# Two halves of the tensor engine in turn: the small fp32 products of an S5 mixer and of attention scores

## The chip, the cores and the metric

The kernel runs on one core of a Trainium2 chip. The metric is the device time of one execution in microseconds (us). A core has a tensor engine (PE, whose weight loads the profile calls PEld), a vector engine (DVE), a scalar engine (ACT), GpSimd (POOL), and SyncE (SP), which issues the DMAs here. Products are written to PSUM; the other engines read them from there.

## What is computed

The reference is a decoder trunk of two layers on 256 tokens of 1024 features. Cut to what matters:

```python
for i in range(DEPTH):                                   # 2
    x = layer_norm(ALPHA * x + 0.5 * swiglu(x, ...))      # feed-forward, 1024 -> 2816 -> 1024
    h = x @ w_in[i]
    z_gmlp, z_qk, z_v, z_s5, z_gate = split(h)
    y_a = gmlp_mixer(z_gmlp, ...)
    y_b = diff_attention(q, k, v, lam, ...)               # 4 heads, two score maps each, causal, 64-wide q and k
    y_c = s5_mixer(z_s5, ...)                             # 32 groups of 16 features, 64 complex states each
    mix = sum_k sigmoid(z_gate[k]) * ((y_a, y_b, y_c)[k] @ w_branch[i, k])
    x = layer_norm(ALPHA * x + mix @ w_out[i])
    x = layer_norm(ALPHA * x + 0.5 * swiglu(x, ...))
```

In `s5_mixer` an input product makes the states' inputs, a linear recurrence over the tokens makes the states, and an output product with a skip term makes y, which goes through a GELU and a gated linear unit (GLU).

## The kernel before, in words

**Products.** Nearly all products are with large weights. A weight tile is split into a high and a low part (`wh` on ACT, `wl` on DVE) and each product is done as three with inputs rounded to fp32r. The small products are left in plain fp32, and each of them stands in the trace as two MATMULs: the S5 input products `bu`, the S5 output products `py`, the attention scores `pss`, and the products with the attention weights `po`.

**Order.** The program has no loop order of its own. Streams (Python generators) yield operations, requests for buffers (`Alloc`) and `Event`s. `Scheduler.run` (L250) keeps a model of each engine's clock and of when each tile is written and read, and merges the streams into one static program; each engine then executes its instructions in that order, waiting on semaphores. A `bundle` (L70) is a group of operations of one engine that is issued without another between. On PE the small streams go ahead of the main stream once their inputs are due; the attention streams have priority 30, the S5 ones 40 (35 for the first step of the scan), the main stream 50.

**PSUM.** The small products share the pool `acc` of four banks (`ps`, L316). A bank comes free when its reader is through.

**The mixer** (L1153). After the products of gMLP, values and the S5 input, the main stream computes q and k (`psq`), then 12 gates (`psg`), four products of the first two branches (`psp`, from `ya` and `yb`), the GLU (`psl`) and the third branch (`psc`), in the order of the list `GATES`. Beside it run three S5 streams and two attention streams:

- `s5_in` (L1034), for each of four feature tiles f: for i = 0 and then i = 1, four products with rows 64 i to 64 i + 63 of `wbf` and `U`, into a bank `bu` of its own.
- `s5_scan` (L1052): DVE turns the inputs (`t`), scans them (`gr`, `gi`) and turns them back into `Hr` and `Hi`.
- `s5_out` (L1105), for each f: state products 64 columns wide with `Hr` (p = 0) and `Hi` (p = 1), for q2 = 0, 1 and i = 0, 1, output partitions 64 i to 64 i + 63; and a direct map for each q2 and i, 32 by 32, on rows 64 i to 64 i + 31 and output partitions 64 i + 32 to 64 i + 63. All of them go into one bank `py`, and the accumulation starts and ends for each q2. The bundles are (q2 = 0, p = 0): state, direct, state, direct; (0, 1): state, state; and the same for q2 = 1. ACT copies `py` into `y`, DVE adds the skip term, and for two tiles at a time GELU and a split give `y5h` and `y5l`, which the GLU reads.
- `head` (L960), one stream for the even and one for the odd heads (e = 0, 1), four heads-and-query-blocks n = 0 to 3 in turn: allocate one bank `pss`, two score products with rows 64 e to 64 e + 63 of q and k (128 keys wide for n = 0, 1; 256 for n = 2, 3), the softmax on DVE and ACT, transposes (`tra`), and `po`. A stream asks for the scores of n + 1 only after `po` of n. `heads_out` normalizes and transposes a query block and gives `ybh` and `ybl`.

Of the kernel before, what the change touches and what calls it, by code (L numbers as in the profile page):

```python
# [31 lines left out]
# The order of the gates (branch, pair of output tiles), of the products of the first two branches (3 + branch, half of  # L32
# the output tiles) and of the GLU.
# [3 lines left out]
# Priorities of the streams (smaller goes first).  # L37
# [8 lines left out]
# Activation tables that hold a function.  # L46
# [3 lines left out]
class Op:  # L50
    """Instructions of one engine that are issued together."""
# [5 lines left out]
class Alloc:  # L57
    def __init__(self, pool, tag, bufs, make):
        self.pool, self.tag, self.bufs, self.make = pool, tag, bufs, make

# [21 lines left out]
class Engine:  # L82
    """Turns a call into an Op with an estimate of its cost."""
# [40 lines left out]
class Scheduler:  # L124
    """Merges streams of operations into one program order.

    Every stream is a generator that yields Ops (issued in its order), Allocs (answered with a tile once a buffer is
    free) and Events (passed once set).  An estimate of each engine's clock and of when each piece of a tile is
    written and read decides which stream goes next."""

# [14 lines left out]
    def spawn(self, gen, prio):  # L145
        p = prio if callable(prio) else (lambda: prio)  # of the stream's other engines; on PE it precedes the main stream
        self.seq += 1
        self.streams.append([gen, p, None, self.seq])

# [73 lines left out]

    def free(self, *tiles):
        for t in tiles:
            name = t[:].tensor.name
            self.slots[self.where.pop(name)].append(float(self.track[name][0].max()))

# [1 line left out]
    def settle(self, s):  # L230
        gen = s[0]
        val = None
        while True:
            h = s[2]
            if isinstance(h, Op):
                return True
            if isinstance(h, Alloc):
                val = self.alloc(h)
                if val is None:
                    return True  # L240
            elif isinstance(h, Event):
                if not h.ok:
                    return True
            try:
                s[2] = gen.send(val)
            except StopIteration:
                return False
            val = None
# [31 lines left out]
class Pair:  # L280
    """Two chunks of the weights: as loaded, and split into two parts."""
# [5 lines left out]
class Trunk:  # L287
# [36 lines left out]
    def slab(self, i, tag, name, dt, bufs):  # L324
        # a pair of chunks, in the ring or in tiles that are idle then
        if i in self.spare:
            tags = self.spare[i].pop(0)
            h = []
            for tg in tags:
                x = yield self.t([128, 1024], tg, name, dt)  # L330
                h.append(x)
            return h, h
        x = yield self.t([128, 2048], tag, name, dt, bufs)
        return [x], [x[:, 0:1024], x[:, 1024:2048]]
# [52 lines left out]
    def xstat(self, out, x, t, pair, i, n):  # L387
        # token tile t of x @ 512 columns; K-tiles 4 i .. 4 i + 3 of 4 n
# [9 lines left out]
    def wstat(self, out, ws, x):  # L398
        # ws: (hi, lo) [128, 128] of each K-tile; out [128, 256]
# [9 lines left out]
    def blocks(self, w, c, j, n):  # L409
        # n K-tiles of 128 columns, from column block j of chunk c  # L410
        return [tuple(z[c][:, 128 * (j + k):128 * (j + k) + 128] for z in (w.hi, w.lo)) for k in range(n)]

    def couple(self, name):
        # two output tiles of the next pair of weight chunks
# [7 lines left out]
    def sums(self, final):  # L422
        # PSUM of a product with 1024 output columns: (columns, tile) for each token tile
# [9 lines left out]
    def kdown(self, acc, h, pair, t, first, last, only=None):  # L433
        # two K-tiles of a product with 1024 output columns, token tile t
# [18 lines left out]
    def rsqrt(self, out, v, eps, tmp):  # L453
        # 1 / sqrt(v + eps) by Newton's iteration; out, v, tmp: [128, 1]
# [8 lines left out]
    def rsqrt_w(self, out, v, eps, tmp):  # L463
        # the same for any width
# [8 lines left out]
    def stats(self, src, n, eps):  # L473
        # mean in column 0, 1 / deviation in column 2
# [8 lines left out]
    def to_xt(self, src, t, gain=None, done=None):  # L483
        # features of token tile t onto partitions, in two parts; gain: (scale, bias) by feature
# [79 lines left out]
    def affine(self, t, x, gb):  # L564
        # gain and bias of the normalized tokens, for the residual
# [18 lines left out]
    def tail(self, n, acc, h, xr, gb, final, first=False):  # L584
        # the last n pairs of K-tiles, token tile 0 ahead of token tile 1
        ps = []
        x_ev = [Event(), Event()]
        for t in range(2):
            if t == 1 and final:
                # by pieces of the columns, for the last normalization to start early  # L590
# [131 lines left out]
    def prep(self, layer, r):  # L722
        """r receives what the mixer of this layer needs."""
# [19 lines left out]
        # minus lambda of the differential attention  # L743
# [18 lines left out]
        # th - 2 pi round(th / 2 pi)  # L762
# [14 lines left out]
        # c = (a - 1) / lambda  # L777
# [13 lines left out]
        # block-diagonal input and output maps  # L791
# [48 lines left out]
        # C, then C a; the imaginary parts negated  # L840
# [23 lines left out]
        # transposes of the input maps, and the direct map of even tokens  # L864
# [25 lines left out]
        # rotation tables: cos and sin of 2 theta c, c = 16 a + b  # L890
# [69 lines left out]
    def head(self, r, qk, va, hs, st):  # L960
        V, A = self.V, self.A
        ts, stt = V.tensor_scalar, V.scalar_tensor_tensor
        for e in [r["ev"]] + st["in"]:
            yield e
        for qb, h in hs:
            ke = 128 * (qb + 1)
            rows = slice(64 * (h % 2), 64 * (h % 2) + 64)
            ps = yield self.ps(self.acc, "pss", (128, 2, 256))
            yield bundle([self.mmul(ps[:, m, 0:ke], qk[0][rows, 2 * m + h // 2, qb * 128:qb * 128 + 128],
                                    qk[1][rows, 2 * m + h // 2, 0:ke], True, True) for m in range(2)])  # L970
# [6 lines left out]
            self.free(ps)  # L977
            yield ts(out=a[:, 2:4], in0=a[:, 0:2], scalar1=-0.125, scalar2=None, op0=ALU.mult)
# [28 lines left out]
        if st["run"] == 0:  # L1007
            self.free(va, *qk)
# [25 lines left out]
    def s5_in(self, r, U2, ev_u, box):  # L1034
        # input products of the four feature tiles
        yield r["ev"]
        yield ev_u
        for f in range(4):
            wb = yield self.t([128, 2, 2, 128], "wbf", "wbf", bufs=2)
            yield self.GQ.dma_start(out=wb, in_=r["wbd"][f // 2][:, 2 * (f % 2):2 * (f % 2) + 2])  # L1040
            if f:
                yield box[f - 1][2]
            for i in range(2):
                rs = slice(64 * i, 64 * i + 64)
                x = yield self.ps(self.acc, f"bu{i}", (128, 2, 2, 128))
                yield bundle([self.mmul(x[:, p, q2, :], wb[rs, q2, p, :], U2[rs, 2 * f + q2, :], True, True)
                              for q2 in range(2) for p in range(2)])
                box[f][i].append(x)
                box[f][i][0].set()
# [55 lines left out]
    def s5_out(self, r, u5, U2, out):  # L1105
# [3 lines left out]
        for f in range(4):  # L1109
# [4 lines left out]
            for q2 in range(2):  # L1114
                j = 2 * f + q2
                for p in range(2):
                    ops = []
                    for i in range(2):
                        q = 2 * q2 + i
                        ops.append(self.mmul(py[64 * i:64 * i + 64, q2, :], cf[:, q, p, :], self.H[p][:, q, :],  # L1120
                                             p == 0, p == 1))
                        if p == 0:
                            ops.append(self.mmul(py[64 * i + 32:64 * i + 64, q2, 0:128],
                                                 r["k0"][64 * i:64 * i + 32, j, :], U2[64 * i:64 * i + 32, j, :],
                                                 False, False))
                    yield bundle(ops)
# [26 lines left out]
    def mixer(self, layer, r):  # L1153
# [57 lines left out]
        # gMLP  # L1211
# [28 lines left out]
        # attention  # L1240
# [13 lines left out]
        st = {"in": qk_ev + va_ev, "po": [None, None], "got": [None, None], "left": [4, 4], "run": 2, "o": o, "yb": yb, "n": 0, "ev": Event()}  # L1254
        for e in range(2):
            s.spawn(self.head(r, qk, va, [(0, e), (0, e + 2), (1, e), (1, e + 2)], st), P_ATT)
# [14 lines left out]
        # gates, and the products of the first two branches  # L1271
# [13 lines left out]
        def branch(b, m2):  # L1285
            # branch b, two pairs of output tiles
# [112 lines left out]
    def main(self):  # L1399
# [21 lines left out]
        def warm():  # L1421
            # keeps the clock of the tensor engine up until the first weights are there
# [59 lines left out]
def pack(inp):  # L1482
    """Lays the weights out in the order in which the tensor engine takes them, and the small arrays by partition."""
# [4 lines left out]
    def rows(w, c0, n):  # x-stationary operand: all K-tiles of n columns, 2048 columns of data per pair  # L1488
        v = w[:, c0:c0 + n].reshape(-1, 128, n).transpose(1, 0, 2)
        for i in range(0, v.shape[1], 4):  # L1490
            chunks.append(v[:, i:i + 4].reshape(128, 2048))

    def cols(w, c0, n):  # weight-stationary operand: tiles [K-tile, 128 columns]
# [43 lines left out]
    def states(v):  # [32 groups, 64 states, ...] -> [(2 groups, states), 16, ...]  # L1537
# [42 lines left out]
```

## Time and profile before

| | |
|---|---|
| median of 3 runs | 1253.62 us (1252.46 to 1255.15) |
| the profiled execution: span, first to last instruction | 1251.0 us |
| PE busy | 1236.9 us, 99% |
| PEld busy | 1140.3 us, 91% |
| DVE busy | 889.1 us, 71% |
| ACT busy | 636.4 us, 51% |
| DMA | 246.18 MB, mean 197 GB/s |

How to read it: busy time is the union of an engine's instructions. Matmuls overlap, so their mean duration is longer than the distance between their starts, and what a group of products costs is read from its first start to the start of what PE does next. The chain of work that ended last goes back from the last instruction to whatever released each step.

### The profile page before, as it was taken

How to read it: one execution, taken by the hardware profiler on the slowest of the kernel's cores; microseconds unless marked ns; L12 is line 12 of the kernel's file. 1: busy time of each engine (PE TensorE's matmuls, PEld its weight loads, DVE VectorE, ACT ScalarE, POOL GpSimd, SP SyncE). 2: the span in 40 equal slices, each digit the busy share in tenths (PEclk: the TensorE clock that was granted, in tenths of full speed). 3: DMA queues.
4: the chain of work that ended last, by engine and by line, in shares of the span. 5: the costliest groups of instructions: out<-in, count | busy, mean ns of one | idle time of the engine just before them, and what ended most of it. 6: DMA issues, size and time to landing. Idle time of an engine off the chain costs nothing.

```text
span 1251.0 us, 21124 instructions
## 1 busy us (share of the span) xinstructions
PE 1236.9 (99%) x8734; PEld 1140.3 (91%) x8734; DVE 889.1 (71%) x1564; ACT 636.4 (51%) x980; POOL 14.8 (1%) x52
## 2 busy tenths in 40 slices
PE   8999999999999999999999999999999999999997
PEld 7999998999999889999889999989998998999996
DVE  6887659769886898775685544695798778754546
ACT  6445537655635564454464343467464366543430
POOL 2000000000000020000000000000000000000000
PEclk9999999999999999999999999999999999999998
DMA  8657654653445565666455554465535464654540
GB/s 311 247 177 258 242 204 170 232 215 110 166 185 209 206 227 203 223 237 216 171 227 189 186 191 180 170 237 204 194 118 186 183 216 155 252 200 175 196 168 34
DMA packets 42864, 246.18 MB, mean 197 GB/s; under 512 B 4880, under 2 KB 5648, under 8 KB 17424
## 3 DMA queue, kind: packets, MB, share of 16 engines
q1 hardware_dynamic: 42768, 244.84, 53.8%
q8 instruction: 68, 1.11, 0.3%
q14 instruction: 28, 0.23, 0.1%
HBM read 233.28 MB, written 11.53 MB: 196 GB/s over the span
## 4 chain that ended last, share of the span: by engine, by line
PE 97%; DVE 2%; ACT 1%; DMA 0%; issue 0%; DVEq 0%
PE ac L196 23%; PE puc L196 17%; PE pgc L196 16%; PE psg L196 12%; PE psq L196 4%; PE psp L196 4%; PE pg L196 3%; PE pu L196 2%; PE py L196 2%; PE psc L196 2%; PE psu L196 2%; PE ps L196 2%; PE pvg L196 2%; PE pva L196 2%; PE bu L196 1%; PE pss L196 1%
## 5 line engine op out<-in xcount | busy, mean ns | idle before, releaser
L196 DVE TENSOR_TENSOR wl<-raw,wh 128x1024 fp32r<-128x1024 f32 (+2 forms) x416 | 481.2, 1189 | 189.1 <-ACT wh L196 174.9
L196 ACT CAST wh<-raw 128x1024 fp32r<-128x1024 f32 (+2 forms) x416 | 410.0, 1023 | 276.3 <-PE ac L196 92.6
L196 PE MATMUL pgc<-xl,wh 128*128 128x256 f32 x576 | 163.7, 284 | 0.0
L196 PE MATMUL puc<-xl,wh 128*128 128x256 f32 x576 | 163.3, 284 | 0.0
L196 PE MATMUL puc<-xh,wl 128*128 128x256 f32 x576 | 163.0, 283 | 0.0
L196 PE MATMUL puc<-xh,wh 128*128 128x256 f32 x576 | 163.0, 283 | 0.0
L196 PE MATMUL pgc<-xh,wl 128*128 128x256 f32 x576 | 163.0, 283 | 0.0
L196 PE MATMUL pgc<-xh,wh 128*128 128x256 f32 x576 | 163.0, 283 | 0.0
L196 PE MATMUL ac<-wh,hTl 128*128 128x512 f32 (+1 forms) x374 | 141.5, 378 | 0.0
L196 PE MATMUL ac<-wh,hTh 128*128 128x512 f32 (+1 forms) x374 | 141.2, 378 | 0.0
L196 PE MATMUL ac<-wl,hTh 128*128 128x512 f32 (+1 forms) x374 | 140.9, 377 | 0.0
L196 PE MATMUL psg<-xl,wh 128*128 128x256 f32 x384 | 112.3, 293 | 0.0
L196 PEld LDWEIGHTS pgc<-xh,wh 128*128 128x128 f32 x576 | 110.4, 192 | 1.0
L196 PEld LDWEIGHTS pgc<-xl,wh 128*128 128x128 f32 x576 | 110.4, 192 | 1.0
L196 PEld LDWEIGHTS puc<-xl,wh 128*128 128x128 f32 x576 | 110.6, 192 | 0.1
L196 PEld LDWEIGHTS puc<-xh,wh 128*128 128x128 f32 x576 | 110.6, 192 | 0.0
L196 PEld LDWEIGHTS puc<-xh,wl 128*128 128x128 f32 x576 | 110.6, 192 | 0.0
L196 PEld LDWEIGHTS pgc<-xh,wl 128*128 128x128 f32 x576 | 110.4, 192 | 0.0
L196 PE MATMUL psg<-xh,wh 128*128 128x256 f32 x384 | 108.6, 283 | 0.0
L196 PE MATMUL psg<-xh,wl 128*128 128x256 f32 x384 | 108.5, 283 | 0.0
L196 PEld LDWEIGHTS ac<-wl,hTh 128*128 128x128 f32 x374 | 70.3, 188 | 13.2
L196 PEld LDWEIGHTS ac<-wh,hTl 128*128 128x128 f32 x374 | 70.4, 188 | 12.3
(263 smaller groups left out, 2355.8 us busy)
## 6 DMA issues: line engine op xcount, KB each, us to landing
raw<-in_wst_dram SPq DMA_DIRECT2D x198, 1024.0 KB, 4.8
raw<-in_wst_dram SPq DMA_DIRECT2D x16, 256.0 KB, 5.1
tbd<-tabw SPq DMA_DIRECT2D x8, 512.0 KB, 6.8
tab<-tbd SPq DMA_DIRECT2D x8, 512.0 KB, 5.6
lng<-in_lngb_dram SPq DMA_DIRECT2D x6, 512.0 KB, 6.4
lnb<-in_lngb_dram SPq DMA_DIRECT2D x6, 512.0 KB, 7.2
wbd<-WB SPq DMA_DIRECT2D x4, 512.0 KB, 8.4
cf<-cd SPq DMA_DIRECT2D x8, 256.0 KB, 6.5
```

The costliest lines, as they stand in the source:

```text
L196: fn(**kw)
```

## The change

The score products move out of `head` into a stream of their own, `scores`, which asks for two banks at once (a new request, `AllocAll`, answered only when both are free) and issues the products of the even and the odd head in one bundle, in turn. It goes on to n + 1 as soon as DVE has read both banks of n. In `s5_in` the products for i = 0 and 1 of a feature tile become one bundle, in turn, again with two banks at once. In `s5_out` all products of a feature tile become one bundle; the four direct maps stand together between the state products, and the bank's accumulation starts with the first state products and ends with the last. The scheduler's model of costs is not changed. The rest of the diff takes out comments.

```diff
+class AllocAll:
+    def __init__(self, parts):
+        self.parts = parts
...
+    def alloc_all(self, parts):
+        a = parts[0]
+        if len(self.slots.setdefault((a.pool.name, a.tag), [0.0] * a.bufs)) < len(parts):
+            return None
+        return [self.alloc(p) for p in parts]
...
-    def head(self, r, qk, va, hs, st):
+    def scores(self, r, qk, hs, st):
+        for e in [r["ev"]] + st["in"]:
+            yield e
+        for n, (qb, j) in enumerate(hs):
+            ke = 128 * (qb + 1)
+            if n:
+                for e in range(2):
+                    yield st["sc"][n - 1][e][2]
+            ps = yield AllocAll([self.ps(self.acc, "pss", (128, 2, 256)) for _ in range(2)])
+            yield bundle([self.mmul(ps[e][:, m, 0:ke], qk[0][64 * e:64 * e + 64, 2 * m + j, qb * 128:qb * 128 + 128],
+                                    qk[1][64 * e:64 * e + 64, 2 * m + j, 0:ke], True, True)
+                          for m in range(2) for e in range(2)])
+            for e in range(2):
+                st["sc"][n][e][0] = ps[e]
+                st["sc"][n][e][1].set()
+        self.free(*qk)
+
+    def head(self, r, va, e, hs, st):
...
-        for qb, h in hs:
+        for n, (qb, j) in enumerate(hs):
             ke = 128 * (qb + 1)
-            rows = slice(64 * (h % 2), 64 * (h % 2) + 64)
-            ps = yield self.ps(self.acc, "pss", (128, 2, 256))
-            yield bundle([self.mmul(ps[:, m, 0:ke], qk[0][rows, 2 * m + h // 2, qb * 128:qb * 128 + 128],
-                                    qk[1][rows, 2 * m + h // 2, 0:ke], True, True) for m in range(2)])
+            h = 2 * j + e
+            yield st["sc"][n][e][1]
+            ps = st["sc"][n][e][0]
...
             self.free(ps)
+            st["sc"][n][e][2].set()
...
+            x = yield AllocAll([self.ps(self.acc, f"bu{i}", (128, 2, 2, 128)) for i in range(2)])
+            rs = [slice(64 * i, 64 * i + 64) for i in range(2)]
+            yield bundle([self.mmul(x[i][:, p, q2, :], wb[rs[i], q2, p, :], U2[rs[i], 2 * f + q2, :], True, True)
+                          for q2 in range(2) for p in range(2) for i in range(2)])
             for i in range(2):
-                rs = slice(64 * i, 64 * i + 64)
-                x = yield self.ps(self.acc, f"bu{i}", (128, 2, 2, 128))
-                yield bundle([self.mmul(x[:, p, q2, :], wb[rs, q2, p, :], U2[rs, 2 * f + q2, :], True, True)
-                              for q2 in range(2) for p in range(2)])
...
-            for q2 in range(2):
-                j = 2 * f + q2
-                for p in range(2):
-                    ops = []
-                    for i in range(2):
-                        q = 2 * q2 + i
-                        ops.append(self.mmul(py[64 * i:64 * i + 64, q2, :], cf[:, q, p, :], self.H[p][:, q, :],
-                                             p == 0, p == 1))
-                        if p == 0:
-                            ops.append(self.mmul(py[64 * i + 32:64 * i + 64, q2, 0:128],
-                                                 r["k0"][64 * i:64 * i + 32, j, :], U2[64 * i:64 * i + 32, j, :],
-                                                 False, False))
-                    yield bundle(ops)
+            def states(q2, p):
+                return [self.mmul(py[64 * i:64 * i + 64, q2, :], cf[:, 2 * q2 + i, p, :], self.H[p][:, 2 * q2 + i, :],
+                                  q2 == p == 0, q2 == p == 1) for i in range(2)]
+            direct = [self.mmul(py[64 * i + 32:64 * i + 64, q2, 0:128], r["k0"][64 * i:64 * i + 32, 2 * f + q2, :],
+                                U2[64 * i:64 * i + 32, 2 * f + q2, :], False, False)
+                      for q2 in range(2) for i in range(2)]
+            yield bundle(states(0, 0) + states(0, 1) + states(1, 0) + direct + states(1, 1))
```

## Rows read from the trace of the kernel before

**Rows 1.** The profile page: its span, and its chain of work that ended last.

```profile
span 1251.0 us, 21124 instructions
...
PE 97%; DVE 2%; ACT 1%; DMA 0%; issue 0%; DVEq 0%
```

**Rows 2.** Stretch, its length; busy PE, PEld, DVE, ACT, POOL; clock, DMA share, GB/s.

```profile
257.00:392.00 135.00, 134.88 (x1087) 124.10 (x1086) 108.71 (x252) 68.65 (x146) 0.00 (x0) 1.00 0.45 165
```

**Rows 3.** PE in order of time (start, duration, what), the first S5 input products.

```profile
257.19 1.71 PE L196 MATMUL bu<-U,wbf 64*128 64x128 f32 x16
258.82 0.39 PE L196 MATMUL psq<-xl,wh 128*128 128x256 f32 x1
```

**Rows 4.** PE in order of time, the first feature tile of the S5 output.

```profile
272.36 0.43 PE L196 MATMUL py<-Hr,cf 128*64 128x129 f32 x2
272.72 0.40 PE L196 MATMUL py<-U,k 32*32 32x128 f32 x2
273.05 0.43 PE L196 MATMUL py<-Hr,cf 128*64 128x129 f32 x2
...
273.75 0.44 PE L196 MATMUL py<-Hi,cf 128*64 128x129 f32 x4
274.02 0.38 PE L196 MATMUL py<-Hr,cf 128*64 128x129 f32 x2
274.33 0.40 PE L196 MATMUL py<-U,k 32*32 32x128 f32 x2
...
275.73 0.39 PE L196 MATMUL psq<-xl,wh 128*128 128x256 f32 x1
```

**Rows 5.** PE in order of time, scores of n = 0, 1, 2 and 3.

```profile
279.52 0.72 PE L196 MATMUL pss<-k,q 64*128 64x128 f32 x8
280.17 0.39 PE L196 MATMUL psg<-xl,wh 128*128 128x256 f32 x1
...
288.61 0.71 PE L196 MATMUL pss<-k,q 64*128 64x128 f32 x4
289.25 0.33 PE L196 MATMUL tra<-ident,sm 128*128 128x128 f32 x1
...
299.65 0.48 PE L196 MATMUL pss<-k,q 64*128 64x256 f32 x1
299.66 0.48 PE L196 MATMUL bu<-U,wbf 64*128 64x128 f32 x2
...
301.79 0.41 PE L196 MATMUL tra<-ident,sm 128*128 128x128 f32 x2
...
308.53 1.13 PE L196 MATMUL pss<-k,q 64*128 64x256 f32 x4
309.59 0.71 PE L196 MATMUL po<-va,at 128*128 128x128 f32 x4
```

**Rows 6.** DVE in order of time: states, turned inputs, and what branch and GLU read.

```profile
271.42 0.69 DVE L196 TENSOR_TENSOR Hi<-u,v 128x512 f32<-128x512 f32 x1
...
319.98 0.69 DVE L196 TENSOR_TENSOR Hi<-u,v 128x512 f32<-128x512 f32 x1
...
330.91 0.68 DVE L196 TENSOR_TENSOR ybl<-tro,ybh 128x512 fp32r<-128x512 f32 x1
...
333.02 1.41 DVE L196 TENSOR_TENSOR t<-bu,tab 128x256 f32<-128x256 f32 x4
...
388.73 0.69 DVE L196 TENSOR_TENSOR y5l<-y,y5h 128x512 fp32r<-128x512 f32 x1
```

**Rows 7.** PE in order of time: output of tile 1, second branch, GLU.

```profile
321.85 0.43 PE L196 MATMUL py<-Hr,cf 128*64 128x129 f32 x2
...
352.09 0.39 PE L196 MATMUL psp<-ybl,wh 128*128 128x256 f32 x1
...
390.40 0.28 PE L196 MATMUL psl<-y5l,wh 128*128 128x256 f32 x1
```

**Rows 8.** Waits over the whole span: who waited for whom, us, times, longest.

```profile
DVE y L196 <- ACT y L196: 21.4, 6, 4.6
```

More of the change, by code (lines that the diff above doesn't have):

```diff
@@ L236, in settle @@
                 return True
-            if isinstance(h, Alloc):
-                val = self.alloc(h)
+            if isinstance(h, (Alloc, AllocAll)):
+                val = self.alloc(h) if isinstance(h, Alloc) else self.alloc_all(h.parts)
                 if val is None:
@@ L958, in gmlp @@
         ev.set()
-    def head(self, r, qk, va, hs, st):
+    def scores(self, r, qk, hs, st):
[15 more added lines that the diff above has]
+    def head(self, r, va, e, hs, st):
         V, A = self.V, self.A
         ts, stt = V.tensor_scalar, V.scalar_tensor_tensor
-        for e in [r["ev"]] + st["in"]:
-            yield e
-        for qb, h in hs:
+        for n, (qb, j) in enumerate(hs):
             ke = 128 * (qb + 1)
-            rows = slice(64 * (h % 2), 64 * (h % 2) + 64)
-            ps = yield self.ps(self.acc, "pss", (128, 2, 256))
-            yield bundle([self.mmul(ps[:, m, 0:ke], qk[0][rows, 2 * m + h // 2, qb * 128:qb * 128 + 128],
-                                    qk[1][rows, 2 * m + h // 2, 0:ke], True, True) for m in range(2)])
+            h = 2 * j + e
+            yield st["sc"][n][e][1]
+            ps = st["sc"][n][e][0]
             sm = yield self.t([128, 2, 256], "sm", "sm", bufs=2)
@@ L1007, in head @@
         if st["run"] == 0:
-            self.free(va, *qk)
+            self.free(va)
     def heads_out(self, r, qb, st):
@@ L1042, in s5_in @@
                 yield box[f - 1][2]
+            x = yield AllocAll([self.ps(self.acc, f"bu{i}", (128, 2, 2, 128)) for i in range(2)])
+            rs = [slice(64 * i, 64 * i + 64) for i in range(2)]
+            yield bundle([self.mmul(x[i][:, p, q2, :], wb[rs[i], q2, p, :], U2[rs[i], 2 * f + q2, :], True, True)
+                          for q2 in range(2) for p in range(2) for i in range(2)])
             for i in range(2):
-                rs = slice(64 * i, 64 * i + 64)
-                x = yield self.ps(self.acc, f"bu{i}", (128, 2, 2, 128))
-                yield bundle([self.mmul(x[:, p, q2, :], wb[rs, q2, p, :], U2[rs, 2 * f + q2, :], True, True)
-                              for q2 in range(2) for p in range(2)])
-                box[f][i].append(x)
+                box[f][i].append(x[i])
                 box[f][i][0].set()
@@ L1254, in mixer @@
         st = {"in": qk_ev + va_ev, "po": [None, None], "got": [None, None], "left": [4, 4], "run": 2, "o": o, "yb": yb, "n": 0, "ev": Event()}
+        hs = [(0, 0), (0, 1), (1, 0), (1, 1)]
+        st["sc"] = [[[None, Event(), Event()] for _ in range(2)] for _ in hs]
+        s.spawn(self.scores(r, qk, hs, st), P_ATT)
         for e in range(2):
-            s.spawn(self.head(r, qk, va, [(0, e), (0, e + 2), (1, e), (1, e + 2)], st), P_ATT)
+            s.spawn(self.head(r, va, e, hs, st), P_ATT)
         zz, z_ev = [], [Event(), Event()]
```

## The prediction

> **What bounds the kernel now.** I read the page first, its span and its chain of work that ended last. The chain is 97% PE, and of 1251.0 us almost nothing is put down to DMA or issue [rows 1]. The profiled execution is 2.6 us under the median of 1253.62; I take the gain from the span and put it on the median. Next come the busy times of the stretch that holds all the small products of the first layer, 257 to 392 us: PE is busy 134.88 of 135 us at a granted clock of 1.00, DVE 108.7 and ACT 68.7 [rows 2]. The second layer repeats the pattern, so everything below is per layer, times two. PE has no idle time to lose: a PE microsecond taken out is a microsecond gained, as long as DVE, with 26.3 us idle, delivers earlier too.
>
> In PE's timeline the reader looks at starts, not durations. A fp32 product shows as two MATMULs; I call them records.
>
> **What a group costs, and whether halves run beside each other.** Scores of n = 0, eight records, four on each row half, take 279.52 to 280.17 = 0.65 us; one head alone (n = 1), four records on one half, takes 0.64 [rows 5]. So the second head was free: two row halves run beside each other if their records are near enough in the queue. The mixed stretch says the same: at 299.65 a score starts and at 299.66 an input product of the other half [rows 5]. In columns, four state records of two column halves (x4, 273.75) last 0.27 until the next start, while two of one half (272.36) last 0.36, including the change to the 32 by 32 maps [rows 4].
>
> A record of 128 columns at the steady rate: four records of 256 columns take 1.06 (308.53 to 309.59), four of 128 take 0.64, so (1.06 - 0.64) / 4 = 0.105 us. The rest, 0.64 - 4 x 0.105 = 0.22, is paid once per group, for entering and leaving it.
>
> **S5 input products.** Sixteen records take 258.82 - 257.19 = 1.63 us [rows 3]. They stand as eight of one half, then eight of the other, and overlap only in the middle: serially they would take 0.22 + 16 x 0.105 = 1.90. In turn, each half has eight: 0.22 + 8 x 0.105 + 0.01 stagger = 1.07. I take 1.08; 0.55 saved per feature tile. For tiles 0, 1 and 3 that is 1.65 per layer. Their readers lose nothing: half 0 ended at about 0.22 + 8 x 0.105 = 1.06 before and does so now.
>
> **Scores and tile 2.** n = 1: two groups of 0.64 (the second head's is alike) become one of 0.65, saving 0.63. n = 3: two of 1.06 become one of 1.07, saving 1.05. n = 2: one head alone took 1.06 as well, the other ran mixed with tile 2's input products from 299.65 to 301.79 = 2.14; together 3.20 becomes 1.07 + 1.08 = 2.15, saving 1.05. n = 0 gains nothing. Sum 2.73 per layer.
>
> **S5 output products.** A feature tile takes 272.36 to 275.73 = 3.37 us [rows 4]. State, direct, state, direct cost 0.36 + 0.33 twice over, because each change between the shapes has its own start and end; only the Hi pair runs on both column halves. In the new order:
> - states (0, 0), both halves: 0.27, as the Hi pair that follows a change of shape;
> - states (0, 1), no change: two records a half, 2 x 0.105 = 0.21;
> - states (1, 0), then the change: 0.31, as from 274.02 to 274.33;
> - four direct maps, two on each corner: 0.33 for the first two records, 2 x 0.105 for the next, 0.01 stagger: 0.55;
> - states (1, 1) and out: 0.36 + 0.01 = 0.37.
>
> The sum is 1.71, and 1.66 is saved. Four tiles: 6.64 per layer, the largest term. Its uncertain item is the direct maps: no row shows two of them next to each other. From below it is 0.55, from above eight records in a row, 0.33 + 6 x 0.105 = 0.96. I take 0.55, since the halves overlapped in every row where both were at hand. The restart of the accumulation only for the first products costs no instruction.
>
> A rule speaks against this item. The Trainium skill, "TensorEngine Tiling (Array Packing)", section Restrictions and Gotchas, says that different row tiles can't access one PSUM bank at the same time, and both direct maps of a pair, on rows from 0 and from 64, write the one bank of `py`. The mixed rows above wrote two different banks, so no trace here answers it. By that rule the item is 0.96.
>
> **Sum and what stands against it.** 1.65 + 2.73 + 6.64 = 11.0 us per layer, 22.0 in all. Fewer entries into small groups (two score groups less, tiles 2 and 3 no longer cut in two) may add 0 to 0.8 in all, left out.
>
> Added waits: a bundle waits for the last of its inputs and for two free banks, and PE's queue behind it is the gate products, which are the whole main work. So I compare arrivals.
> - First output tile: PE comes 1.1 earlier (two input groups). Hi ends at 271.42 + 0.69 = 272.11 [rows 6], and py started at 272.36; its first Hi product now comes 0.27 into the group, at about 271.5. Stall about 0.6, unless other work is put there: 0 to 0.7.
> - Second output tile: PE comes 1.1 - 0.6 + 1.66 + 2.73 = 4.9 earlier than 321.85 [rows 7]. Hi of that tile ends at 320.67 [rows 6], so 1.2 to 1.4 of that is free; the other 3.5 must come from DVE. DVE lost up to 3.7 us of the kind "waits for y, which waits for ACT's copy of py" before the scores (21.4 us in six waits, 3.6 each [rows 8]), which falls with the first output tile. I charge 0.4, from 0 to 1.5.
> - GLU: `y5l` ends at 389.42 [rows 6], `psl` starts at 390.40 [rows 7]: 0.98 slack. Its chain starts from the last `py`, which gets shorter by 1.66 itself, so no charge.
>
> Stalls: 1.0 per layer, 2.0 in all, bounds 0 and 4.4. The net is 20.0 and the time 1253.6 - 20.0 = 1233.6. Best case: 22.8, 1230.8. A different static order, which the scheduler will draw up with new bundles, may put 2 or 3 us on either side.
>
> **Rivals.**
> 1. *The direct maps run one after another*, because two row groups don't write one bank at once. Each tile costs 0.41 more, 3.3 in all: **1236.9**. For: no row shows it. Against: they write different partitions, and column halves did share that bank. Chance 0.14. This is also the time by the rule of the Trainium skill above.
> 2. *DVE sets the time between the first scores and the second output.* It is busy 108.7 of 135 us [rows 2]; taking 11 out of PE leaves 124, so DVE must be busy 88% in an in-order queue that mixes weights, softmax and scan. If half of the gain becomes PE waits for Hi or `y5l`: 1253.6 - 11 = **1242.6**. For: 0.98 us slack at the GLU. Against: much of DVE's idle time is waiting for PE itself. Chance 0.14.
> 3. *Slower, by the pairs of banks.* Four banks serve scores, `po`, `bu` and `py`. If tile 2's input pair takes two and both `po` of the query blocks one each, scores n = 3 find no two free ones until the second `bu` half has been turned in part, at about 333.7 (half of the x4 from 333.02 [rows 6]) where the scores stood at 308.53 [rows 5]: 25.2 us late. `ybl` ended at 331.59 [rows 6] and its branch started at 352.09 [rows 7], 20.5 slack, of which the earlier PE takes 9.4. Beyond 11.1 us PE waits one for one: 14.1 per layer, 28.2 in all: **1261.8**. It decides from 11.1 us on and costs more than the whole gain from 21.1 us on. Against: with attention waiting, DVE gets to the turn earlier, and so does the bank; the scheduler knows of both. Chance 0.06.
> 4. *The gain is handed back at once*: every wait saved on PE reappears at the next input of DVE, or the halves don't stay beside each other over a longer run: about **1252**. Against: the starts side by side in [rows 4, 5], and the switches saved in py, which need no overlap. Chance 0.04.
>
> **How the numbers follow.** Forecast 0.62, with a range of its own of 1229 to 1238. It is the likeliest, so 1233.6 is the prediction. The range reaches from the best case with some luck in the order, 1228, to rival 2 with its middle, 1243, which leaves out rivals 3 and 4, a tail of rival 2 and a little of the forecast. About 0.2% (2.5 us) is what a measurement of this kernel can tell from no change. Faster by more than that: 0.62 + 0.14 + 0.14 = 0.90; within: 0.04; slower: 0.06.
>
> **What the profile after would show.** Right: `bu` x16 with the next start 1.1 us on; `pss` only as x8, 0.65 and 1.07; `py` of a tile in 1.7, with U,k as one x8 of 0.55 between; PE busy still 99% and few new PE waits. Wrong in rival 1: that x8 near 0.96. Wrong in rival 2: PE waits for Hi or `y5l`, or gaps ahead of `psl`. Rival 3: a late `ybl` and a gap ahead of its `psp`. It would also be wrong if the planner cut the groups up or put them among more `tra` and `po`, with an entry and an exit for each.

## The result, and the profile after

The changed kernel takes 1230.07 us, median of four runs (1229.78 to 1230.82), against 1253.34 (1252.46 to 1255.15): ratio 0.9815, interval 0.9802 to 0.9827. It is 23.3 us faster and 3.5 us under the predicted 1233.6, inside the range and a little better than the "best case" of the text, 1230.8. The profiled execution has a span of 1228.1 us, 22.9 less than before.

The page of the changed kernel, its span and two of its engines, and the stretch of the first layer that holds the small products (columns as in [rows 2]):

```profile
span 1228.1 us, 21124 instructions
...
PE 1214.4 (99%) x8734; PEld 1127.6 (92%) x8734; DVE 886.3 (72%) x1564; ACT 636.8 (52%) x980; POOL 16.2 (1%) x52
```

```profile
257.00:381.20 124.20, 124.12 (x1091) 118.57 (x1090) 108.32 (x252) 69.10 (x147) 0.00 (x0) 1.00 0.50 180
```

The reader is to see that PE lost 22.5 us of busy time with the same number of instructions, and that it is still busy all through the stretch, at a clock of 1.00. DVE did the same work (108.3 us beside 108.7 in [rows 2]) in 10.8 us less.

PE in order of time (start, duration, what), the groups that answer to [rows 3], [rows 4], [rows 5] and [rows 7]:

```profile
257.78 1.16 PE L203 MATMUL bu<-U,wbf 64*128 64x128 f32 x16
258.87 0.39 PE L203 MATMUL psq<-xl,wh 128*128 128x256 f32 x1
...
272.58 0.44 PE L203 MATMUL py<-Hr,cf 128*64 128x129 f32 x4
272.85 0.39 PE L203 MATMUL py<-Hi,cf 128*64 128x129 f32 x4
273.07 0.39 PE L203 MATMUL py<-Hr,cf 128*64 128x129 f32 x4
273.39 0.63 PE L203 MATMUL py<-U,k 32*32 32x128 f32 x8
273.94 0.44 PE L203 MATMUL py<-Hi,cf 128*64 128x129 f32 x4
274.32 0.39 PE L203 MATMUL psq<-xl,wh 128*128 128x256 f32 x1
...
277.38 0.72 PE L203 MATMUL pss<-k,q 64*128 64x128 f32 x8
278.03 0.39 PE L203 MATMUL psg<-xl,wh 128*128 128x256 f32 x1
...
296.65 1.13 PE L203 MATMUL pss<-k,q 64*128 64x256 f32 x8
297.72 0.44 PE L203 MATMUL tra<-ident,sm 128*128 128x128 f32 x2
...
379.75 0.28 PE L203 MATMUL psl<-y5l,wh 128*128 128x256 f32 x1
```

From start to next start: `bu` 1.09 (1.63 before), `pss` 0.65 and 1.07 for both heads, `py` 1.74 (3.37 before). All eight feature tiles and all eight score groups have these values. From the first `bu` to the first `psl` it was 390.40 - 257.19 = 133.21 us and is 379.75 - 257.78 = 121.97: 11.24 less per layer, 22.5 of the 22.9 us of the span.

The whole list of PE's waits in the changed kernel (who waited for whom: us, times, longest):

```profile
PE trx L203 <- DMA x<-in_x_dram: 4.1, 2, 3.6
PE pg L203 <- DVE xl L203: 0.3, 1, 0.3
```

Neither `py`, `psl` nor `psp` is among them. So the two questions for the experiments are whether the groups got cheaper for the reason given, and why no stall came.

### The profile page after: what moved, and what is told of

It is laid out like the page before. It is cut to its first block, busy times and chain, and to the rows that moved or that the text cites. A ratio compares the mean times of both kernels' runs of the same rounds, so it can differ in the third digit from the quotient of the medians.

```text
span 1228.1 us, 21124 instructions
## 1 busy us (share of the span) xinstructions
PE 1214.4 (99%) x8734; PEld 1127.6 (92%) x8734; DVE 886.3 (72%) x1564; ACT 636.8 (52%) x980; POOL 16.2 (1%) x52
## 4 chain that ended last, share of the span: by engine, by line
PE 97%; DVE 2%; DMA 0%; ACT 0%; issue 0%; DVEq 0%; SPq 0%
PE ac L203 23%; PE puc L203 17%; PE pgc L203 17%; PE psg L203 11%; PE psq L203 4%; PE psp L203 4%; PE pg L203 4%; PE pu L203 3%; PE psc L203 2%; PE psu L203 2%; PE ps L203 2%; PE pvg L203 2%; PE pva L203 2%; PE py L203 1%; PE psl L203 1%; PE trx L203 1%
## 5 line engine op out<-in xcount | busy, mean ns | idle before, releaser
L203 PEld LDWEIGHTS ac<-wl,hTh 128*128 128x128 f32 x374 | 70.3, 188 | 13.1
```

What stands on the lines that cost most here:

```text
L203: fn(**kw)
```

## Experiments

The theory, T: two row halves run beside each other when their records are near in the queue, also into one PSUM bank; a PE microsecond taken out is a microsecond gained as long as DVE delivers. The rival, R, is the prediction's second: DVE and what it waits for set the time, so that part of the gain comes back as a wait ahead of the GLU. Each run has the kernel before beside it on the same chip, with a median of 1253.33 to 1253.70.

### One part of the change at a time

**out_alone**: the kernel before with the new `s5_out` only.

> The kernel before with the new S5 output alone. Theory (each group's own price on PE is the whole effect): a feature tile's py takes 1.74 us as in the profile of the changed kernel, instead of 3.37, eight tiles, 13.1 us, and up to 0.8 more for tiles no longer cut in two: 1239.5 us. Rival (part of the gain needs the others, or is taken back by a wait for Hi): 1243 or more.

Measured: 1248.25 us, ratio 0.9959 (0.9944 to 0.9974). `py` takes 1.738 in every tile, as in the whole change, but 8 of some 13 us are lost. PE's timeline at the GLU, with the idle time and its releaser in brackets, and PE's clock around it:

```profile
387.97 0.58 PE L203 MATMUL psl<-y5l,wh 128*128 128x256 f32 x1 [3.29 <-DVE y5l L203]
388.35 0.41 PE L203 MATMUL psl<-y5h,wh 128*128 128x256 f32 x1
388.57 0.41 PE L203 MATMUL psl<-y5h,wl 128*128 128x256 f32 x1
```

```profile
384.00:388.00 4.00, 0.71 (x7) 0.50 (x6) 2.30 (x4) 3.51 (x5) 0.00 (x0) 0.95 0.09 39
388.00:395.00 7.00, 7.00 (x48) 7.00 (x49) 2.44 (x3) 1.88 (x5) 0.00 (x0) 0.79 0.60 225
```

PE waits 3.29 us for `y5l`, and for about 3 us behind the wait its matmuls start 0.21 apart instead of 0.12: at a granted clock of 0.79 a part of that stretch is at the lower level, 1.2 GHz. The `psl` group takes 10.57 us instead of 5.65, so 4.92 per layer and 9.8 in all (more than what is missing; the rest of the new order gave a little back). R has come true here. What is late shows on SP's queue and on DVE:

```profile
366.47 5.73 SPq L203 DMA_DIRECT2D raw<-in_wst_dram  x2
372.25 0.42 SPq L203 DMA_DIRECT2D cf<-cd  x1
```

```profile
372.36 0.68 DVE L203 TENSOR_TENSOR Hi<-u,v 128x512 f32<-128x512 f32 x1
```

The last tile's `Hi` is ready at 373.04, but its `py` starts at 379.81: the coefficients `cf` are asked for behind two weight loads, at 372.25, and land 5.0 us later. PE shows no wait there, since the static order has gate products ahead of that `py`.

**in_alone**: the kernel before with the new `s5_in` only.

> The kernel before with the new S5 input alone. Theory: 1.09 instead of 1.64 us for tiles 0, 1 and 3, 3.3 us in both layers; tile 2, which shared its time with a score group before, gives 0 to 1.1 more: 1249 to 1250 us. Rival (the pair of banks delays the S5 chain, and PE waits at the GLU): 1253 or more.

Measured: 1249.42 us, 0.9971 (0.9961 to 0.9981). The term is confirmed: tiles 0, 1 and 3 at 1.09; the products of tile 2 still run mixed with a score.

**scores_alone**: the kernel before with `scores` only.

> The kernel before with the new stream of scores alone. Theory: 0.63 for n = 1, 1.05 each for n = 2 (unless its second head still runs beside input products) and n = 3, and 0.2 for each group of scores less: 4.5 to 6.5 us in both layers, 1247 to 1249 us. Rival (two banks held early starve the S5 stream): no gain, 1253 or more. If the three parts are independent, their gains sum to the 23.3 us of the whole change.

Measured: 1250.28 us, 0.9973 (0.9963 to 0.9983): a gain, but less than the 4.5 us at least that were expected. Scores take 0.645 and 1.065, but tile 2's `bu` now stands as two groups of 1.085 with a `po` between them (313.93 and 315.65), with no score to run beside. The three parts gain 5.1 + 3.9 + 3.0 = 12.0 us one by one and 23.3 together: what each is worth depends on the others, by the order that the scheduler draws up and by whether the GLU waits.

**out_scores**: the changed kernel with the old `s5_in`.

> The changed kernel with the old S5 input. Theory (the stream of scores, by moving attention ahead on DVE, is what lets the S5 output's gain through): 0.55 more for each of eight input groups, 4.4 us: 1234.5 us, no wait at the GLU. Rival (it needs all three parts, or chance of the order): PE waits at the GLU, 1240 or more.

Measured: 1237.23 us, 0.9873 (0.9856 to 0.9889): 7.2 us over the whole change, between the two. No wait at the GLU. Three tiles cost 0.55 more each, and tile 2, again cut in two around a `po`, costs 2 x 1.085 - 1.09 = 1.08: 2.7 per layer, 5.5 of the 7.2 us. The other 1.7 I don't trace.

### What makes the halves run beside each other

Each product is two records, so "in turn" means two records of one half, then two of the other.

**in_blocks**: all eight records of one half, then the other eight, in one bundle.

```diff
-  for q2 in range(2) for p in range(2) for i in range(2)])
+  for i in range(2) for q2 in range(2) for p in range(2)])
```

> The changed kernel, its input products in one bundle and with two banks still, but eight records of one row half and then eight of the other. Theory (halves overlap only as far as PE looks ahead in its queue): a group goes back to 1.64 us, 0.55 more in each of eight, 4.4 us: 1234.5 us. Rival (the one bundle and the pair of banks are what helps): 1.09 us and 1230 us as with the products in turn.

**blocks_four**: in all three places four records of one half, then four of the other.

```diff
-  for m in range(2) for e in range(2)])                    # scores
+  for e in range(2) for m in range(2)])
-  for q2 in range(2) for p in range(2) for i in range(2)]) # s5_in
+  for q2 in range(2) for i in range(2) for p in range(2)])
-  for q2 in range(2) for i in range(2)]                    # direct maps
+  for i in range(2) for q2 in range(2)]
```

> The changed kernel with four records of one half and then four of the other, in the scores, the S5 input and the direct maps; the states are left in turn. Theory (PE looks some four records ahead, and halves run beside each other within that): the same prices, 0.65 and 1.07 for scores, 1.1 for the input, 0.55 for the direct maps: 1230 to 1231 us. Rival (only strict turns overlap): the input goes to 1.6, the scores of 256 keys to 1.5 or more, the direct maps to 0.75: 1238 or more.

Measured: in_blocks 1234.55 us, 0.9849 (0.9832 to 0.9865); blocks_four 1231.51, 0.9826 (0.9811 to 0.9841). The `bu` groups, first of in_blocks and then of blocks_four:

```profile
257.54 1.71 PE L203 MATMUL bu<-U,wbf 64*128 64x128 f32 x16
259.18 0.39 PE L203 MATMUL psq<-xl,wh 128*128 128x256 f32 x1
```

```profile
258.86 1.26 PE L203 MATMUL bu<-U,wbf 64*128 64x128 f32 x16
260.05 0.39 PE L203 MATMUL psq<-xl,wh 128*128 128x256 f32 x1
```

Blocks of eight take 1.64, as in [rows 3]: the single bundle and the pair of banks bring nothing, the order does. Blocks of four take 1.19, only 0.10 more than in turn; scores 0.652 and 1.072, and `py` 1.745, stay as they were within 0.01. The time of blocks_four is 0.5 us over what was expected, which lies within its interval. Against the 1.90 estimated for serial records, blocks of eight gain 0.26. Read singly in the trace of in_blocks, the starts show how. Counted from the first, they make two series of the same steps, which I take for the two halves: one starts at 0, 0.21, 0.33, 0.44, 0.55, 0.66, 0.77 and 0.88 us, the other at 0.55, 0.77, 0.88 and on to 1.44. So the first record of the second half starts beside the fifth of the first half, ahead of three older ones. In blocks of four it starts 0.01 behind the very first. PE reached some four records ahead in these groups.

### The direct maps

**direct_apart**: the products as in the change, but the direct maps in two places.

```diff
-  bundle(states(0, 0) + states(0, 1) + states(1, 0) + direct + states(1, 1))
+  bundle(states(0, 0) + direct[:2] + states(0, 1) + states(1, 0) + direct[2:] + states(1, 1))
```

> The changed kernel with the direct maps of q2 = 0 after the states (0, 0) and those of q2 = 1 after (1, 0), both in turn as before. Theory (a change of shape costs about 0.2 us of draining and loading each way, and the maps need their own start): a tile goes from 1.74 to about 2.0 us, 2.2 us in all: 1232.3 us. Rival (what helps is the turn alone, standing together nothing): 1230 us.

Measured: 1232.79 us, 0.9835 (0.9820 to 0.9850). Each pair of direct maps:

```profile
273.11 0.41 PE L203 MATMUL py<-U,k 32*32 32x128 f32 x4
273.44 0.44 PE L203 MATMUL py<-Hi,cf 128*64 128x129 f32 x4
```

Four records on two corners take 0.33, what two on one corner took in [rows 4]; `py` takes 2.008, 0.27 more than with all four together. So the second place costs 0.27, and the halves run side by side in both places.

**old_order**: one bundle per tile, in the order of before (state, direct, state, direct, state, state).

> The changed kernel, its S5 output in one bundle still, but in the order of before: state, direct, state, direct, then the Hi pair. Theory (the order alone makes the price): a tile goes from 1.74 back to 3.37 us, 1.63 in each of eight, 13.1 us: 1243.1 us. Rival (the bundle that isn't cut gives a good part): 1241 or less.

Measured: 1243.12 us, 0.9920 (0.9905 to 0.9935); `py` 3.371 as before. Of the 13.0 us between the orders, 4 x 2 x 1.633 = 13.1 are the `py` groups alone. The single bundle is worth nothing.

**padded**: the direct maps padded with zeros to all 128 rows and 64 columns, so that the shape doesn't change; `cf` has one buffer, for room.

```diff
-  k0 = yield self.t([128, 8, 32], "k0", "k0")
+  k0 = yield self.t([128, 8, 2, 64], "k0", "k0")
+  yield self.G.memset(ap=k0, constant=0.0)
...
-  yield A.copy(out=k0[64 * i:64 * i + 32], in_=pk0[64 * i:64 * i + 32])
+  yield A.copy(out=k0[64 * i:64 * i + 32, :, i, 32:64], in_=pk0[64 * i:64 * i + 32])
...
-  cf = yield self.t([128, 4, 2, 64], "cf", "cf", bufs=2)
+  cf = yield self.t([128, 4, 2, 64], "cf", "cf", bufs=1)
...
-  self.mmul(py[64 * i + 32:64 * i + 64, q2, 0:128], r["k0"][64 * i:64 * i + 32, 2 * f + q2, :],
-            U2[64 * i:64 * i + 32, 2 * f + q2, :], False, False)
+  self.mmul(py[64 * i:64 * i + 64, q2, 0:128], r["k0"][:, 2 * f + q2, i, :],
+            U2[:, 2 * f + q2, :], False, False)
```

> The changed kernel with the direct maps widened by zeros to the shape of the state products, 128 rows and 64 columns, so that no shape changes inside a tile's group; cf has one buffer for two, to make room. Theory (what is left above 0.11 us a record is the two changes of shape): a tile's 12 records per half take 0.16 + 10 x 0.11 + 0.2 = 1.46 us for 1.74, 2.2 us in all: 1227.8 us. Rival (the wider maps cost more than the changes of shape, or one cf buffer makes the S5 chain late): 1230 or more.

Measured: 1229.01 us, 0.9807 (0.9792 to 0.9822): 1.1 us under the change, which these intervals don't tell apart. `py` is cheaper for certain:

```profile
274.33 0.61 PE L203 MATMUL py<-U,k 128*64 128x128 f32 x8
274.77 0.39 PE L203 MATMUL py<-Hi,cf 128*64 128x129 f32 x4
```

It takes 1.468 instead of 1.738, in all tiles: 0.27 for one change of shape and back, 2.2 us in all. From the first `bu` to `psl` it is 120.84 us, 1.13 less than the change; the first `bu` comes 1.04 later (258.82), once, so the span is 1227.1.

### What the gain hangs on

**out_cf**: out_alone, with `cf` of tile f + 2 asked for right behind `py` of tile f.

The two lines that go from the loop make up `load`, which puts each `cf` on the list `cfs`.

```diff
...
+  yield from load(0)
+  yield from load(1)
   for f in range(4):
-      cf = yield self.t([128, 4, 2, 64], "cf", "cf", bufs=2)
-      yield self.GQ.dma_start(out=cf, in_=r["cd"][f // 2][:, 4 * (f % 2):4 * (f % 2) + 4])
+      cf = cfs.pop(0)
...
       self.free(cf)
+      if f < 2:
+          yield from load(f + 2)
```

> The new S5 output alone, as in the run of that part, but the maps cf of feature tile f + 2 are asked for as soon as py of tile f is through, and not after the skip term of tile f + 1. In the run without this, cf of tile 3 was issued at 372.25 us and landed some 6.5 later, py stood at 379.81 though Hi ended at 373.04, and PE waited at the GLU, 4.9 us per layer. Theory (the late load of cf is what took the gain back): no wait at the GLU, 1238 to 1240 us. Rival (DVE as a whole is too late for an earlier PE, whatever the load): PE waits on, 1245 or more.

Measured: 1243.42 us, 0.9920 (0.9905 to 0.9935), between the two. The wait is gone: `y5l` ends at 382.82, `psl` starts at 387.00, and PE waits for it no longer. That bears out `cf` as what was late in out_alone, though the order of the rest moved too. The gain is 4.8 us and not the 9.8 of the wait, since the new order gave other things up, among them: scores of n = 0 no longer meet (two groups of 0.638 at 279.48 and 281.02) and tile 2's `bu` is cut in two.

**scan_twice**: the changed kernel with each of the DVE's scans of the S5 done twice into the same output, some 10.4 us of DVE more per layer.

```diff
-  for q in range(4):
+  for q in (0, 1, 2, 3, 0, 1, 2, 3):
```

> The changed kernel with each of the scans done twice on DVE, the second time over the same output: about 2.6 us more DVE work per feature tile, 10.4 per layer, in the S5 chain. PE's work is the same. DVE is busy 108.3 of 124.2 us between the first input products and the GLU, and y5l ends 1.6 us ahead of the GLU's first product. Theory (PE sets the time, DVE's idle time covers most): 1230 to 1240 us, what appears shows as a wait at the GLU. Rival (DVE is as good as full): 20 us appear, 1250 us.

Measured: 1256.06 us, 1.0020 (1.0010 to 1.0030): 26.0 us over the change, more than either expected. PE's waits, and its clock behind them:

```profile
PE py L203 <- DVE Hr L203: 7.3, 2, 3.6
PE psl L203 <- DVE y5l L203: 6.6, 2, 3.3
...
PE py L203 <- DVE Hi L203: 2.8, 2, 1.5
```

```profile
384.00:389.00 5.00, 4.30 (x26) 2.92 (x26) 2.91 (x3) 1.44 (x6) 0.00 (x0) 0.50 0.46 157
389.00:400.00 11.00, 7.72 (x46) 7.69 (x46) 2.56 (x4) 3.42 (x9) 0.00 (x0) 0.61 0.43 176
```

The waits are (7.3 + 6.6 + 2.8) / 2 = 8.4 us per layer, 16.7 in all. The rest is the lower clock level: at 0.50 (1.2 GHz) 4.30 busy us lose 2.2, and from 392.31 to 397.60 matmuls start 0.21 apart instead of 0.12, which loses 5.3 x (1 - 0.12 / 0.21) = 2.3; together 4.5 per layer, 9 in all, and 16.7 + 9 = 25.7 of the 28.1 us between the two profiled spans (1256.2 and 1228.1; this profiled run is 1.9 over its median). The 8.4 us of waiting and the 1.6 us of slack that the changed kernel has at the GLU (below) make 10.0 of DVE's 10.4 us more. DVE's idle time covers hardly any of them: from the first `bu` to the end of `y5l` it is busy 106.4 of 120.3 us in the changed kernel (13.9 idle) and 120.3 of 133.5 us here (13.1 idle).

**after_cf**: the changed kernel with the early `cf` of out_cf.

> The changed kernel with the maps cf of feature tile f + 2 asked for as soon as py of tile f is through. Theory (in the whole change the load of cf isn't late: it is issued at 362.5 us, Hi of tile 3 ends at 368.8, py stands at 370.0, and PE doesn't wait at the GLU): no change, 1229 to 1231 us, unless the order shifts. Rival (cf still costs): 1228 or less.

Measured: 1247.64 us, 0.9955 (0.9940 to 0.9970): 17.6 us over the change. Both expectations missed. Every small group of the first layer has the price of the change, but PE waits at the GLU:

```profile
386.76 0.58 PE L203 MATMUL psl<-y5l,wh 128*128 128x256 f32 x1 [5.75 <-DVE y5l L203]
```

The `psl` group takes 13.57 us instead of 5.65: 7.9 per layer, 5.75 of them waiting and the rest at the lower clock (0.71 from 387 to 394), 15.8 of the 17.6 us. SP's queue shows what moved, first after_cf and then the changed kernel:

```profile
317.21 6.14 SPq L203 DMA_DIRECT2D raw<-in_wst_dram  x2
323.41 0.43 SPq L203 DMA_DIRECT2D tab<-tbd  x1
```

```profile
316.87 0.33 SPq L203 DMA_DIRECT2D raw<-in_wst_dram  x1
317.24 0.47 SPq L203 DMA_DIRECT2D tab<-tbd  x1
```

`tab`, the table by which `bu` is turned, has one buffer. Its load lands 5.7 to 5.8 us after its issue, and DVE's first turn of tile 2 starts at 329.82 in after_cf and at 323.00 in the change, each right behind that. For tile 3 the load is asked for at 349.55 against 340.58. Tile 3's `Hi` ends at 376.71 instead of 368.78, and `y5l` at 386.7 instead of 378.1. Two things set the time of that load: when the one buffer comes free, and what stands ahead in SP's queue. The buffer's last reader on DVE is the second `v` of tile 1, first in after_cf and then in the changed kernel:

```profile
319.09 0.68 DVE L203 TENSOR_TENSOR v<-gi,tab 128x512 f32<-128x512 f32 x1
```

```profile
313.25 0.69 DVE L203 TENSOR_TENSOR v<-gi,tab 128x512 f32<-128x512 f32 x1
```

From the end of `v` to the issue of `tab` it is 3.64 us in after_cf and 3.30 in the changed kernel. So for tile 2 it is DVE's order that makes the load late (5.8 of 6.2 us), and hardly the queue; for tile 3 DVE's last `v` ends 6.3 us later (346.87 against 340.56), and 2.7 of the 9.0 are the queue, where `tab` stands behind a weight load. Asking for `cf` earlier moved the whole static order, and this is what came of it for the last states. That `tab` alone makes the 17.6 us is argued from the two traces; no run moved it by itself.

## Why the prediction was right, point by point

The gain was forecast at 20.0 us and is 23.3. Of the 3.3 us between them 2.0 are stalls that didn't come, 0.5 is the difference in the stretch with the small products (22.5 against 22.0), and 0.8 lies outside it and between span and median.

**Price of a group.** Right to 0.1 us everywhere: `bu` 1.08 forecast and 1.09 measured, scores 0.65 and 1.07, `py` 1.71 and 1.74. With the measured values the three sums are 1.64, 2.73 and 6.53 = 10.9 per layer against 11.0. blocks_four and in_blocks show that it is the distance in the queue that decides, as read from [rows 3, 5]; direct_apart and padded that each entry into another shape costs its own start and end (0.27).

**The direct maps.** The uncertain item was 0.55 or 0.96. It is 0.55 (273.39 to 273.94). The Trainium skill, "TensorEngine Tiling (Array Packing)", section Restrictions and Gotchas, where different row tiles can't use one PSUM bank at once, would have given 0.96: the trace doesn't agree for these products, which lie on rows from 0 and from 64 and write different partitions of the one bank. Rival 1 is out.

**Entries left out.** "0 to 0.8 in all" was right in size: 11.24 measured less 10.91 is 0.33 per layer, 0.7 in all. The reason was right in part. That tiles 2 and 3 were cut in two had cost nothing (1.39 + 1.98 = 3.37, as for a whole tile). Summed from start to next start between the first `bu` and the first `psl`, it is the products with the attention weights that got cheaper, 2.27 us instead of 2.89: four pairs of `po` records that stood right ahead of scores took 0.31 each and now take 0.14. All other products together take 0.28 more.

**Stalls.** This is the term that was mis-sized: 1.0 per layer, 0 measured. That nothing came is due to the static order, which the text allowed for but did not foresee; as far as the two output tiles go, it was luck. DVE in order of time, to be read beside [rows 6]:

```profile
270.88 0.69 DVE L203 TENSOR_TENSOR Hi<-u,v 128x512 f32<-128x512 f32 x1
...
319.53 0.68 DVE L203 TENSOR_TENSOR Hi<-u,v 128x512 f32<-128x512 f32 x1
...
322.40 0.68 DVE L203 TENSOR_TENSOR ybl<-tro,ybh 128x512 fp32r<-128x512 f32 x1
323.00 0.75 DVE L203 TENSOR_TENSOR t<-bu,tab 128x256 f32<-128x256 f32 x2
...
368.10 0.68 DVE L203 TENSOR_TENSOR Hi<-u,v 128x512 f32<-128x512 f32 x1
...
377.42 0.69 DVE L203 TENSOR_TENSOR y5l<-y,y5h 128x512 fp32r<-128x512 f32 x1
```

At the first output tile 0.6 was charged "unless other work is put there", and it was. The chain that ended last, from `bu` of tile 1 on, before and then after:

```profile
267.92 4.51 PE psq L196 x36
272.43 1.64 PE py L196 x9
```

```profile
267.42 5.23 PE psq L203 x42
272.65 1.36 PE py L203 x19
```

42 records of q and k stand there instead of 36; `py` starts at 272.58, with `Hi` ready at 271.57.

At the second output tile the text asked DVE to come 3.5 us earlier, "charged 0.4". `Hi` came only 0.5 earlier (ready at 320.21 instead of 320.67), so that step was wrong: the wait of DVE's `y` for ACT's copy of the first `py`, which the text counted on, fell only from 3.71 to 3.44 us. PE didn't wait all the same: that `py` starts at 321.02, only 0.8 earlier than in [rows 7], since the static order put more gate products ahead of it (288 records since the first `bu`, 258 before). The order moved something else too: tile 2's input products, which need two banks, stand 11 us later than in [rows 5].

```profile
310.94 1.16 PE L203 MATMUL bu<-U,wbf 64*128 64x128 f32 x16
...
321.02 0.33 PE L203 MATMUL py<-Hr,cf 128*64 128x129 f32 x2
```

It is not the delay by pairs of banks of which rival 3 spoke, though it looks like it. In in_alone the input asks for pairs too, and tile 2's `bu` starts at 299.28; in scores_alone it has single banks and starts at 313.93. `s5_in` asks for tile 2's products only behind tile 1's last scans (`gi`), and DVE comes to these 11 us later, behind attention's work, which the stream of scores brought forward. Before and after:

```profile
298.69 0.73 DVE L196 TENSOR_TENSOR_SCAN gi<-pk,t 128x128 f32<-128x128 f32 x2
```

```profile
310.09 0.73 DVE L203 TENSOR_TENSOR_SCAN gi<-pk,t 128x128 f32<-128x128 f32 x2
```

In both kernels, and in in_alone, scores_alone and out_scores, `bu` starts 0.1 to 0.3 us behind the end of these. The later place costs nothing: DVE reads them from 323.00 on, and before the change it did from 333.02 [rows 6]. And attention, which rival 3 had late, is early: `ybl` ends at 323.1 instead of 331.6.

At the GLU no charge was made, and none came: `y5l` ends at 378.11, `psl` starts at 379.75. The slack is 1.64 us, and the reason given was too easy: that the chain gets shorter with `py`. In out_alone `py` got shorter as well, and the GLU waited 3.29 us.

**Rival 2.** It didn't happen, but its place and its price are real: at the GLU, for `y5l`, 4.9 us per layer in out_alone, 7.9 in after_cf. The argument against it, that much of DVE's idle time is waiting for PE, held for this change: DVE's idle time fell from 26.3 to 15.9 us with PE's gain, and no wait came. But what is left of it is no reserve, as scan_twice shows. With `cf` asked for earlier, and the order that followed from it, the change stands at 1247.6. So the chance of 0.14 was if anything too low, and "2 or 3 us on either side" for the order much too low.

**Rival 4.** Out: 23.3 us came, and every group kept its price.

## What to carry to other kernels

Small products on row or column halves gain as long as the two halves stand within a few records of each other in PE's queue, and products of one shape belong together, since a change of shape and back cost 0.27 us here, more than two records. When PE time is taken out of a kernel that is bound by PE, look first for the chain whose slack is smallest at the next join (here `y5l`, 1.6 us), and for what its loads wait for, a buffer or the queue that they share; how busy the other engine is says little. Where a scheduler draws up the order, a part's worth is not its worth alone (12.0 us against 23.3 here).

## What the runs showed of the hardware that was not expected

Products on rows from 0 and from 64 that write different partitions of one PSUM bank ran side by side: the four direct maps took 0.55 us, where one after the other they would take an estimated 0.96. PE started products of another row half ahead of older ones, some four records ahead: groups of 16 records take 1.09 us in turn, 1.19 in blocks of four, 1.64 in blocks of eight. A wait of 3.29 us on PE cost 4.92 (out_alone), and one of 5.75 cost 7.92 (after_cf). Most of the difference is that the matmuls behind it start 0.21 us apart instead of 0.12, for 2.9 us in the one and 4.2 us in the other, at the lower clock level of 1.2 GHz.
